# A ring of 20 weight tiles with six lent ones, and conditioning weights in loads of 1 MB

## The chip, the cores and the metric

The kernel runs on one core of a Trainium2 chip. The metric is the device time of one execution in microseconds, and the table below gives the median of three executions. One more execution was profiled; all rows shown here are from its trace.

## What is computed

One layer of a decoder trunk for 1024 tokens of width 1024, with a conditioning vector c. Token mixing is a projection into a convolution branch and a state-space (scan) branch; channel mixing is a mixture of 64 experts, of which each token uses two.

```python
mod = silu(c) @ w_ada + b_ada                       # 1024 x 6144
sh1, sc1, g1, sh2, sc2, g2 = split(mod, 6)
h = x * (1 + sc1) + sh1
conf_val, conf_gate, z, xbc, dt = split(h @ w_in)
u = silu(layer_norm(conv31(conf_val * sigmoid(conf_gate))))
y = gated_rmsnorm(ssd_scan(silu(conv4(xbc)), dt), z)
x = layer_norm(ALPHA * x + g1 * (concat(u, y) @ w_out))      # ln1
h = x * (1 + sc2) + sh2
ffn = sum over a token's two experts of gate * ((silu(h @ w1) * (h @ w3)) @ w2)
x = layer_norm(ALPHA * x + g2 * ffn)                         # ln2, the output
```

Each expert has 6 MB of weights (w1, w3, w2), 64 experts 384 MB.

## The kernel before

**Phase one** (to about 925 us). `ada_steps(r)` computes a third of `mod` each: r = 0 (sh1, sc1) at the start, since nothing goes without it, r = 1 and 2 (the other four vectors) as generators, of which `ada_more` takes a step whenever a block of projection weights is loaded. A product there has the 1024 x 2048 weights of its third as moving operand and the conditioning vector, repeated over 32 columns, as stationary one; four such products, at column offsets 0, 32, 64, 96 of the array (`tile_position`), fill the four parts of one PSUM bank. `wada` names the weight tiles, `pm` or `ada` the bank, `badd` the bias. The bank is one of a few that the projections (`mm_bank`) use too.

The tokens are worked in two halves, h = 0 and 1. `make_h(h)` transposes x and writes the modulated h as a high and a low part (hTh, hTl) in 8 tiles of 128 x 512 each. Then blocks of 128 columns of w_in are loaded (`load_block`, names wg, wv, wx, wz), split into high and low parts on ACT and POOL in the first half and kept in DRAM (`wind`) for the second, and multiplied (names pg, pv, px, pz on PE, three products for each of 8 k). Convolution taps run on DVE, the scan on PE, DVE and ACT. The out-projection passes with `wo` follow (700 to 925 us), then the routing tables (925 to 968 us), whose result for the four places that can be loaded early are the lists fix_i and fix_l.

**Expert phase** (968 to 1955 us). Expert weights come through a ring of N_RING tiles of 1 MB, loaded from SP's queue in the order of `plan`, 384 loads of 1 MB. Load n goes into tile n % N_RING and is issued when the products of load n - N_RING are done. The first N_EARLY loads need only fix_i; the next wait for fix_l. The places (experts or parts of them) are grouped into units, whose kinds stand in ORDER: F (the fixed ones), S (four places side by side, 24 loads), L (two, 12), T and H (three or one for the crowded experts). A unit gathers its tokens (`gather`, xg), transposes them (xT), multiplies with w1 (h0) and w3 (h1), joins them (s1), transposes (hT), multiplies with w2 (yp), scales by the gate (ys, yl, yh) and sends the rows to `ybuf` in DRAM. The last unit (S, number 60) does not send; its rows go through products with one-hot matrices (`hot`) straight into the last sums.

**Sums and end.** `acc` holds 8 tiles of 128 x 1024. `load_sum(i)` loads the normalized rows of phase one (`td`) from ACT's queue into tile i, multiplies by ln1's weight, adds ln1's bias (both on DVE, the vectors in l1) and scales by ALPHA on ACT. Before, one follows each of units 4 to 11. `tc.keep_in_program_order` holds its loads and its first DVE operation to the order in which the program is written; everything else is placed on its engine's queue by a scheduler. At the end `collect` gathers the rows of ybuf for each of 8 token tiles (`yb` for the first, free ring tiles for the others), and `finish` adds them to acc (DVE), sums in PSUM (z), takes statistics (BN_STATS, bs), normalizes and writes out.

The functions that the change touches, with the line numbers of the profile:

## Time and profile before

| | us |
|---|---|
| median of three executions | 2002.7 (2000.44 to 2003.66) |
| the profiled execution | 2007.87, span 2006.1 |
| phase one and routing | 0 to 968 |
| expert phase, to the last y | 968 to 1955 |
| end: last sums, normalization, output | 1955 to 2006.1 |

PE is busy 89% of the span, DVE 48%, ACT 28%, POOL 25%. A share over the whole span mixes these stages; what limits a stage is read from its own window. PE is TensorE, DVE VectorE, ACT ScalarE, POOL GpSimd, SP the engine whose queue issues most loads.

### The profile page before, as it was taken

Reading aid. Unit: us, or ns where it says so; the run is one execution under the profiler, and the core shown is the slowest. Engines: PE = TensorE matmul, PEld = TensorE weight load, DVE = VectorE, ACT = ScalarE, POOL = GpSimd, SP = SyncE. Lnnn points to the kernel's source line nnn. Section 1 sums busy time; section 2 is a strip of 40 time slices with the busy share of each in tenths; the row PEclk is TensorE's granted clock in tenths of the full one; section 3 lists DMA queues with packets and bytes.
Section 4 is the critical chain, followed back from the end, with each engine's and each line's share of the span. In section 5 each row is a group of like instructions: output and inputs, shape, how many; then the busy total and the mean of one; then the engine's idle time right before and its main releaser. Section 6 shows DMA issues by size and latency. Waiting matters only on the chain.

```text
span 2006.1 us, 23809 instructions
## 1 busy us (share of the span) xinstructions
PE 1789.1 (89%) x8136; PEld 998.1 (50%) x8136; DVE 956.2 (48%) x1928; ACT 557.4 (28%) x1054; POOL 501.6 (25%) x408
## 2 busy tenths in 40 slices
PE   6899999899999999997879799788898997999786
PEld 1566667587788777886323133232242331443233
DVE  1699999869998997867113012112011110111117
ACT  0345554643555465644100011011010010111001
POOL 0457656513443465311100001000000000000014
PEclk7899999889999999998889899999999998999998
DMA  7788888656655446674899999999989999999993
GB/s 242 234 293 265 260 254 300 223 195 212 203 190 192 160 150 221 218 289 163 316 419 419 420 415 354 419 419 420 420 300 391 419 420 419 418 412 371 419 366 161
DMA packets 202328, 620.81 MB, mean 309 GB/s; under 512 B 25886, under 2 KB 91702, under 8 KB 154332
## 3 DMA queue, kind: packets, MB, share of 16 engines
q1 hardware_dynamic: 155792, 551.74, 71.8%
q10 hardware_dynamic: 36188, 42.34, 6.6%
q0 software_dynamic: 10224, 25.18, 3.3%
q8 instruction: 65, 1.06, 0.2%
q14 instruction: 59, 0.48, 0.1%
HBM read 575.07 MB, written 79.25 MB: 326 GB/s over the span
## 4 chain that ended last, share of the span: by engine, by line
PE 45%; DMA 31%; DVE 11%; issue 5%; ACT 4%; POOL 3%; ACTq 0%; SPq 0%; DVEq 0%; POOLq 0%
DMA ring<-in_expert_w_dram 25%; PE mix L480 6%; PE px L480 5%; PE h0h L1332 3%; DVE ac L605 2%; PE pg L480 2%; PE h1h L1332 2%; PE pv L480 2%; PE pz L480 2%; PE yph L1351 2%; PE yps L1351 2%; PE ypl L1351 2%; PE h1l L1332 2%; PE h0l L1332 2%; PE ypt L1351 1%
## 5 line engine op out<-in xcount | busy, mean ns | idle before, releaser
L605 DVE SCALAR_TENSOR_TENSOR ac<-u,cw,ac 128x512 f32<-128x512 f32 x394 | 295.7, 750 | 5.5
L1294 POOL DMA_INDIRECT xg<-td,gidx x32 | 32.9, 1027 | 754.8 <-PE tph L1302 206.7
L480 PE MATMUL px<-hTh,wx_hl 128*128 128x512 f32 x512 | 169.8, 401 | 1.6 <-DVE u L619 1.2
L1332 PE MATMUL h1s<-ring,xTs 128*32 128x512 f32 x512 | 105.2, 733 | 43.2 <-DMA ring<-in_expert_w_dram 43.2
L480 PE MATMUL mix<-wo_hl,cth 128*128 128x512 f32 x416 | 129.9, 405 | 1.7 <-ACT zs L726 1.1
L1351 PE MATMUL yps<-ring,hTs 128*32 128x512 f32 x512 | 109.1, 613 | 19.3 <-DMA ring<-in_expert_w_dram 16.8
L1338 DVE TENSOR_TENSOR s1s<-s1s,h1s 128x512 f32<-128x512 f32 x8 | 5.5, 688 | 220.8 <-PE h1s L1332 220.8
L480 PEld LDWEIGHTS px<-hTh,wx_hl 128*128 128x128 f32 x512 | 95.6, 188 | 30.4 <-issue 4.6
L454 POOL TENSOR_TENSOR wo_hl<-wo,wo_hl 128x512 fp32r<-128x512 f32 x52 | 74.0, 1436 | 113.3 <-ACT wo_hl L453 106.1
L480 PE MATMUL px<-hTl,wx_hl 128*128 128x512 f32 x256 | 101.3, 396 | 0.0
L480 PE MATMUL pg<-hTh,wg_hl 128*128 128x512 f32 x256 | 89.2, 419 | 2.0 <-DVE h L520 1.8
L480 PEld LDWEIGHTS mix<-wo_hl,cth 128*128 128x128 f32 x416 | 78.2, 190 | 22.0 <-DVE wo_hl L454 1.5
L1332 PE MATMUL h0s<-ring,xTs 128*32 128x512 f32 x512 | 75.4, 639 | 14.0 <-DMA ring<-in_expert_w_dram 14.0
L311 PE MATMUL ada<-wada,cond 128*32 128x512 f32 x192 | 67.7, 706 | 19.7 <-DMA wada<-in_w_ada_dram 19.7
L480 PE MATMUL pv<-hTh,wv_hl 128*128 128x512 f32 x256 | 84.0, 396 | 0.0
L480 PE MATMUL pz<-hTh,wz_hl 128*128 128x512 f32 x256 | 83.6, 397 | 0.1
L1332 PEld LDWEIGHTS h1s<-ring,xTs 128*32 128x32 f32 x512 | 22.6, 129 | 121.0 <-DMA ring<-in_expert_w_dram 76.6
L480 PE MATMUL mix<-wo_hl,ctl 128*128 128x512 f32 x208 | 77.6, 404 | 3.1 <-DVE ctl L962 3.1
L453 ACT CAST wo_hl<-wo 128x512 fp32r<-128x512 f32 x104 | 62.9, 617 | 33.0 <-PE mix L480 18.1
L1351 PEld LDWEIGHTS yps<-ring,hTs 128*32 128x32 f32 x512 | 26.7, 111 | 87.4 <-issue 46.4
L1351 PE MATMUL ypl<-ring,hTl 128*64 128x512 f32 x256 | 66.6, 598 | 2.3 <-ACT hTl L1344 2.3
L1332 PE MATMUL h0l<-ring,xTl 128*64 128x512 f32 x256 | 63.6, 598 | 3.9 <-DMA ring<-in_expert_w_dram 3.9
(622 smaller groups left out, 3465.5 us busy)
## 6 DMA issues: line engine op xcount, KB each, us to landing
ring<-in_expert_w_dram SPq DMA_DIRECT2D x384, 1024.0 KB
wo<-in_w_out_dram SPq DMA_DIRECT2D x112, 256.0 KB
wada<-in_w_ada_dram SPq DMA_DIRECT2D x96, 256.0 KB
wind<-wx_hl SPq DMA_DIRECT2D x32, 512.0 KB
wx_hl<-wind SPq DMA_DIRECT2D x32, 512.0 KB
wind<-wg_hl SPq DMA_DIRECT2D x16, 512.0 KB
wind<-wv_hl SPq DMA_DIRECT2D x16, 512.0 KB
wx<-in_w_in_dram SPq DMA_DIRECT2D x32, 256.0 KB
```

The lines of the kernel that those rows point to most:

```text
L311: nc.tensor.matmul(pm[32 * j:32 * j + 32, :], lhs, wt, start=(k == 0), stop=(k == KT - 1), tile_position=(0, 32 * j))
L453: nc.scalar.copy(hi, wt)
L454: (eng or nc.gpsimd).tensor_tensor(lo, wt, hi, op=OP.subtract)
L480: nc.tensor.matmul(pt, lhs[a_], rhs[b_], start=(first and n == 0), stop=(last and n == 2))
L605: nc.vector.scalar_tensor_tensor(to, v_, w_, run_, op0=OP.mult, op1=OP.add)
L1294: nc.gpsimd.indirect_dma_start(out=t_, out_offset=None, in_=td, in_offset=bass.IndirectOffsetOnAxis(ap=gcol, axis=0), bounds_check=T - 1, ...
L1332: nc.tensor.matmul(hp[a:b, :], xT[:, 4 * hf + k, a:b], w_[:, k, :], start=(hf + k == 0), stop=(hf + k == 4), tile_position=(0, a))
L1338: nc.vector.tensor_tensor(s1, s1, hps[1], op=OP.mult)
L1351: nc.tensor.matmul(yps[n][a:b, :], hT[:, 2 * hf + k, a:b], w_[:, k, 512 * n:512 * n + 512], start=(hf + k == 0), stop=(hf + k == 2), tile_ ...
```

## The change

Ring: 20 tiles instead of 14, of which 14 are the ring's own and six are lent: a tile `lent`, the four halves (2 x 1024 columns x 2) of `acc`, and a tile `lend` that the last unit's one-hot matrices use. The last 44 loads (N_BACK) keep to the 14. Since acc is lent, all eight `load_sum` stand behind the unit that is third from the end. The two vectors l1 and later the first gathered rows lie in `lent` instead of `yb`. A list `slot`, `before` takes the place of n % N_RING. 16 instead of 13 loads go out on fix_i.

Conditioning: 8 loads of 1 MB for each third, with the four products of one load side by side, instead of 32 loads of 256 KB. The first third goes through the buffers of hT (four tiles of 1 MB, in which hTh and hTl now lie as slices), the second and third through one buffer `wada`, and only in the second half of the tokens. Some small loads move from ACT's queue to POOL's, the bias of the first third is loaded ahead, and the loads of mod_row wait for a store. In half 0, odd tiles of h are made with one more operation on ACT and one less on DVE.

```diff
-N_RING = 14
-N_RING_A = 8
-N_EARLY = 13
+N_RING = 20
+N_RING_A = 10
+N_EARLY = 16
+N_LEND = 6
+N_BACK = 44
...
-HA = "00000000,00000000".split(",")
+HA = "01010101,00000000".split(",")
...
         def ada_steps(r):
 
+            def load_bias():
+                t_ = wk.tile([P, 512], F32, tag="sq", bufs=SQB, name=f"badd{r}")
+                nc.scalar.dma_start(t_, bass.AP(tensor=b_ada.tensor, offset=b_ada.offset + r * 2048,
+                                                ap=[[512, 4], [0, 32], [1, 512]]))
+                return t_
+            badd = load_bias() if r == 0 else None
             pm = mm_bank(f"ada{r}")
             for k in range(KT):
+
+                if r == 0 and k != 4:
+                    wt = big.tile([P, 2048], F32, tag="hT", bufs=4, name=f"wada{r}_{k}")
+                else:
+                    wt = wk.tile([P, 2048], F32, tag="wada", bufs=1, name=f"wada{r}_{k}")
+                nc.sync.dma_start(wt, w_ada[k * P:(k + 1) * P, r * 2048:(r + 1) * 2048])
                 lhs = cond[:, k:k + 1].to_broadcast([P, 32])
-                for q in range(2):
-                    for j in (2 * q, 2 * q + 1):
-
-                        pool, tag, bufs = ([(wst, "w", WB)] * (1 if r else WB)
-                                           + [(cat, "cu", 8)] * 8 + [(cat, "cy", 8)] * 8)[0 if r else (4 * k + j) % (WB + 16)]
-                        wt = pool.tile([P, 512], F32, tag=tag, bufs=bufs, name=f"wada{r}_{k}{j}")
-                        nc.sync.dma_start(wt, w_ada[k * P:(k + 1) * P, r * 2048 + j * 512:r * 2048 + (j + 1) * 512])
-                        nc.tensor.matmul(pm[32 * j:32 * j + 32, :], lhs, wt,
-                                         start=(k == 0), stop=(k == KT - 1), tile_position=(0, 32 * j))
+                for j in range(4):
+                    nc.tensor.matmul(pm[32 * j:32 * j + 32, :], lhs, wt[:, 512 * j:512 * j + 512],
+                                     start=(k == 0), stop=(k == KT - 1), tile_position=(0, 32 * j))
```

```diff
-        def ada_more(n):
-            n = n if skip[0] % 3 else 0
-            skip[0] += 1
-            while n > 0 and late:
-                if next(late[0], 0) == 0:
-                    late.pop(0)
-                n -= 1
+        def ada_more(h):
+
+            if h == 1 and late and next(late[0], 0) == 0:
+                late.pop(0)
 
...
+    lent = rt2.tile([P, 2048], F32, name="lent")
...
+        ring += [ringb.tile([P, 2048], F32, name=f"ring{j}") for j in range(N_RING_A, N_RING - N_LEND)]
+        ring += [lent] + [acc[:, 2 * j:2 * j + 2, :].rearrange("p a d -> p (a d)") for j in range(4)] + [None]
         load_fixed(ring, N_RING_A, N_EARLY, fix_i)
...
+        ring[N_RING - 1] = wk.tile([P, 2048], F32, tag="lend", bufs=1, name="lend")
...
         def load_sum(i):
 
             if i == 0:
-                l1_ = wk.tile([P, 2, D], F32, tag="yb", bufs=1, name="l1")
-                l1[:] = [l1_[:, 0], l1_[:, 1]]
+                l1[:] = [lent[:, 0:D], lent[:, D:2 * D]]
                 for t_, v_ in zip(l1, (ln1_g, ln1_b)):
                     tc.keep_in_program_order(nc.scalar.dma_start(t_, bc(v_, 0, D)))
...
-                yy = wk.tile([P, 2, D], F32, tag="yb", bufs=1, name="yb") if i == 0 else spare[i].rearrange("p (k d) -> p k d", k=2)
+                yy = (spare[i] if i else lent).rearrange("p (k d) -> p k d", k=2)
                 nc.gpsimd.dma_start(yy, ybuf[2 * i * P:2 * (i + 1) * P, :].rearrange("(t k) d -> t k d", k=2))
```

```diff
-                hot = wk.tile([P, HW, P], F32R, tag="hot", bufs=1, name=f"hot{nm}_{j}")
+                held = wk.tile([P, 2048], F32R, tag="lend", bufs=1, name="held")
+                hot = held[:, 0:HW * P].rearrange("p (j t) -> p j t", t=P)
...
             for n in range(2):
-                yh, yl = (wk.tile([P, 512], F32R, tag=f"y{p_}", bufs=2, name=f"y{p_}{nm}_{n}") for p_ in "hl")
+                yh, yl = held[:, D + 512 * n:D + 512 * n + 512], yls[:, half[n]]
                 nc.scalar.copy(yh, y[:, half[n]])
                 nc.vector.tensor_tensor(yl, y[:, half[n]], yh, op=OP.subtract)
...
-                if n >= N_RING and uses[n - N_RING] > 0:
+                if before[n] is not None and uses[before[n]] > 0:
...
-                    load(ring[n % N_RING], *place_regs(r), which, hf)
+                    load(ring[slot[n]], *place_regs(r), which, hf)
...
+        slot, before = [], []
+        turn = [(s_, None) for s_ in range(N_RING)]
+        for n in range(len(plan)):
+            while n >= len(plan) - N_BACK and turn[0][0] >= N_RING - N_LEND:
+                turn.pop(0)
+            s_, b_ = turn.pop(0)
+            slot.append(s_)
+            before.append(b_)
+            turn.append((s_, n))
         emitted()
...
             unit(nm, [tiles(r) for r in places], cols_of(u))
-            if 4 <= n < 12:
-                load_sum(n - 4)
...
-        spare = [ring[(len(plan) + j) % N_RING] for j in range(N_RING)]
+            if n == len(units) - 3:
+                for i in range(8):
+                    load_sum(i)
...
+        spare = [ring[s_] for s_, _ in turn]
```

What the order of instructions on three engines shows. First PE in the second half of the tokens, before, where the projection px1_8 passes into px1_12 (name, then half 1 and the block; hTh and hTl the operands, whl the weights):

```order
L480 MATMUL px1_8_3967<-hTl1_6_3424,wx1_8_1_hl_3965 128x512
L480 MATMUL px1_8_3967<-hTh1_6_3420,wx1_8_1_hl_3965 128x512
L480 MATMUL px1_8_3967<-hTh1_7_3431,wx1_8_1_hl_3965 128x512
L480 MATMUL px1_8_3967<-hTl1_7_3435,wx1_8_1_hl_3965 128x512
L480 MATMUL px1_8_3967<-hTh1_7_3431,wx1_8_1_hl_3965 128x512
L480 MATMUL px1_12_4011<-hTh1_0_3348,wx1_12_0_hl_4001 128x512
L480 MATMUL px1_12_4011<-hTl1_0_3352,wx1_12_0_hl_4001 128x512
L480 MATMUL px1_12_4011<-hTh1_0_3348,wx1_12_0_hl_4001 128x512
```

The same place in the changed kernel (ada1 and ada2 are the banks of the second and third thirds, wada1_6 the load of k = 6):

```order
L485 MATMUL px1_8_3756<-hTh1_4_3162,wx1_8_1_hl_3754 128x512 x2
L321 MATMUL ada1_3379<-wada1_5_3619,cond_192 32x512 x4
L485 MATMUL px1_8_3756<-hTl1_4_3163,wx1_8_1_hl_3754 128x512
L485 MATMUL px1_8_3756<-hTh1_4_3162,wx1_8_1_hl_3754 128x512 x2
L485 MATMUL px1_8_3756<-hTl1_4_3163,wx1_8_1_hl_3754 128x512
L485 MATMUL px1_8_3756<-hTh1_4_3162,wx1_8_1_hl_3754 128x512
L321 MATMUL ada1_3379<-wada1_6_3629,cond_192 32x512 x4
L321 MATMUL ada1_3379<-wada1_7_3737,cond_192 32x512 x4
L321 MATMUL ada2_3791<-wada2_0_3792,cond_192 32x512 x4
L485 MATMUL px1_12_3801<-hTh1_0_3120,wx1_12_0_hl_3790 128x512
L485 MATMUL px1_12_3801<-hTl1_0_3121,wx1_12_0_hl_3790 128x512
```

Three groups of four conditioning products (wada1_6, wada1_7, wada2_0) now stand back to back between px1_8 and px1_12, five projection products behind wada1_5; each has a load of its own into the one buffer.

SP's queue at the start of the expert phase, before: ring8 to ring12 go out on fix_i, ring13 and what follows behind TENSOR_LOAD fix_l.

```order
L246 TENSOR_LOAD fix_i_105
L243 ISA
L243 DMA ring12_8652<-in_expert_w1_dram 128x2048
L246 TENSOR_LOAD fix_l_8638
L243 ISA
L243 DMA ring13_8653<-in_expert_w1_dram 128x2048
L246 TENSOR_LOAD fix_l_8638
L243 ISA
L243 DMA ring0_6719<-in_expert_w1_dram 128x2048
L246 TENSOR_LOAD fix_l_8638
```

In the changed kernel:

```order
L248 TENSOR_LOAD fix_i_105
L245 ISA
L245 DMA ring13_8488<-in_expert_w1_dram 128x2048
L245 ISA
L245 DMA lent_8465<-in_expert_w1_dram 128x2048
L245 ISA
L245 DMA acc_8464<-in_expert_w1_dram 128x2048
L248 TENSOR_LOAD fix_l_8475
L245 ISA
L245 DMA acc_8464<-in_expert_w3_dram 128x2048
L248 TENSOR_LOAD fix_l_8475
L245 ISA
```

ring13, lent and the first half of acc now stand ahead of the load of fix_l; three halves of acc and lend follow it.

ACT's queue over the last unit (s60), before: s1 and hT of the unit, the vectors of ln2, the copies of the last y, and the square root of the first statistics (rs0).

```order
L1309 ACTIVATE xTl30_12330<-tpl30_0_12331,modc_106 128x128 x4
L1337 ACTIVATE s1l30_12403<-h0l30_12349 128x512
L1344 COPY hTl30_12411<-thl30_12406 128x512
L1309 ACTIVATE xTs60_12444<-tps60_0_12445,modc_106 128x128 x4
L1337 ACTIVATE s1s60_12539<-h0s60_12463 128x512
L1590 DMA ring6_8112<-in_ln2_g_dram 128x1024
L1591 DMA ring6_8112<-in_ln2_b_dram 128x1024
L1344 COPY hTs60_12547<-ths60_12542 128x512
L1372 CAST yhs60_0_12590<-ys60_12583 128x512
L1372 CAST yhs60_1_12594<-ys60_12583 128x512
L1565 ACT_TABLE_LOAD
```

In the changed kernel, from behind the last unit's hT on (DMA acc<-td is a load of `load_sum`, ACTIVATE acc its scaling; three scalings and three loads stand ahead of this piece):

```order
L1282 DMA acc_8464<-td_86 128x1024
L1381 CAST held_12428<-ys60_12423 128x512 x2
L1285 ACTIVATE acc_8464<-acc_8464 128x1024
L1282 DMA acc_8464<-td_86 128x1024
L1285 ACTIVATE acc_8464<-acc_8464 128x1024
L1282 DMA acc_8464<-td_86 128x1024
L1285 ACTIVATE acc_8464<-acc_8464 128x1024
L1282 DMA acc_8464<-td_86 128x1024
L1285 ACTIVATE acc_8464<-acc_8464 128x1024
L1282 DMA acc_8464<-td_86 128x1024
L1285 ACTIVATE acc_8464<-acc_8464 128x1024
L1584 ACT_TABLE_LOAD
```

Loads and scalings of acc alternate there; five scalings and four loads stand behind the copies of the last y (held), ahead of the table load for the square root.

## Rows read from the trace of the kernel before

**Rows 1.** The page's slices of the span (40 equal ones), transfers only.

```profile
DMA  7788888656655446674899999999989999999993
GB/s 242 234 293 265 260 254 300 223 195 212 203 190 192 160 150 221 218 289 163 316 419 419 420 415 354 419 419 420 420 300 391 419 420 419 418 412 371 419 366 161
```

**Rows 2.** The page's chain that ended last, by line, share of the span.

```profile
DMA ring<-in_expert_w_dram 25%; PE mix L480 6%; PE px L480 5%; PE h0h L1332 3%; DVE ac L605 2%; PE pg L480 2%; PE h1h L1332 2%; PE pv L480 2%; PE pz L480 2%; PE yph L1351 2%; PE yps L1351 2%; PE ypl L1351 2%; PE h1l L1332 2%; PE h0l L1332 2%; PE ypt L1351 1%
```

**Rows 3.** Busy time by stage, with clock, DMA share and rate.

```profile
core 0: us, PE busy (x) PEld busy (x) DVE busy (x) ACT busy (x) POOL busy (x), PEclk, DMA share, GB/s
0.00:50.00 50.00, 31.20 (x82) 7.96 (x82) 5.94 (x57) 2.96 (x4) 0.87 (x8) 0.80 0.77 242
...
66.00:404.00 338.00, 316.90 (x1500) 224.44 (x1500) 297.39 (x490) 168.98 (x297) 194.88 (x152) 0.97 0.78 255
100.00:300.00 200.00, 187.27 (x883) 133.52 (x882) 187.19 (x307) 103.48 (x185) 120.43 (x93) 1.00 0.83 268
404.00:700.00 296.00, 290.53 (x1508) 232.25 (x1507) 257.37 (x483) 137.88 (x238) 103.39 (x85) 0.98 0.60 195
...
925.00:968.00 43.00, 26.06 (x154) 18.93 (x156) 25.07 (x103) 14.35 (x27) 3.25 (x3) 0.64 0.44 163
968.00:1955.00 987.00, 860.39 (x3662) 316.72 (x3662) 142.26 (x302) 90.03 (x196) 68.80 (x68) 0.97 0.99 402
```

**Rows 4.** The same view of stretches of the expert phase.

```profile
980.00:1000.00 20.00, 20.00 (x96) 7.55 (x92) 2.78 (x6) 0.81 (x2) 2.02 (x2) 1.00 1.02 418
1200.00:1240.00 40.00, 38.58 (x137) 16.01 (x138) 12.09 (x19) 6.45 (x13) 6.02 (x4) 1.00 0.88 338
1460.00:1520.00 60.00, 57.73 (x229) 24.25 (x230) 8.87 (x19) 5.78 (x13) 6.11 (x6) 1.00 0.82 298
1800.00:1840.00 40.00, 38.53 (x172) 15.49 (x170) 6.24 (x13) 3.19 (x7) 4.07 (x4) 1.00 0.91 352
1920.00:1940.00 20.00, 19.71 (x132) 7.03 (x134) 2.87 (x6) 2.59 (x6) 1.56 (x2) 1.00 0.78 292
```

**Rows 5.** Waits of SP's queue: us in total, times, longest us.

```profile
SPq L243 <- DMA ring<-in_expert_w_dram: 503.5, 254, 11.5
...
SPq L246 <- DVE fix_l L1320: 33.6, 1, 33.6
...
SPq L243 <- PE h0t6x L1332: 17.0, 2, 13.2
```

**Rows 6.** The chain in the first 70 us: start, us, what.

```profile
33.58 8.33 DMA mod_row<-in_ln_g_dram
...
41.99 2.79 DMA wada<-in_w_ada_dram
44.78 0.04 issue
44.82 3.93 PE ada L311 x6
```

**Rows 7.** Line L311 alone from 57 to 404 us, and PE's timeline (start, us).

```profile
57.00:404.00 347.00, 37.59 (x128) 5.12 (x128) 0.97 0.79 258
...
388.30 1.94 PE L311 MATMUL ada<-wada,cond 128*32 128x512 f32 x8
390.17 1.06 PE L499 MATMUL xT<-ident,x 128*128 128x128 f32 x4
391.16 1.04 PE L311 MATMUL ada<-wada,cond 128*32 128x512 f32 x2
```

**Rows 8.** Lines of load_sum (ns min/median/max), and a gather of 0.5 MB in the chain.

```profile
L1275 ACTq DMA_DIRECT2D acc<-td x8: 326/327/353, 1158.8 to 1351.7; - x8
...
L1276 DVE TENSOR_TENSOR acc<-acc,l x8: 1215/1216/1226, 1175.0 to 1378.1; 128x1024 f32<-128x1024 f32 x8
...
L1277 DVE TENSOR_TENSOR acc<-acc,l x8: 1215/1224/1226, 1176.3 to 1379.4; 128x1024 f32<-128x1024 f32 x8
...
L1278 ACT ACTIVATE acc<-acc x8: 1047/1056/1066, 1179.9 to 1380.7; 128x1024 f32<-128x1024 f32 x8
...
954.83 3.90 DMA xg<-td,gidx
```

**Rows 9.** The end: chain and DVE's timeline (start, us), and an issue with its landing.

```profile
1944.78 0.70 DVE s1s L1338
...
1955.00 0.75 DVE L1356 SCALAR_TENSOR_TENSOR ys<-yps,gslot,g_bc 128x512 f32<-128x512 f32 x1 [9.53 <-PE yps L1351]
1955.67 1.22 DVE L1556 TENSOR_TENSOR acc<-acc,yb 128x1024 f32<-128x1024 f32 x1
...
1959.80 0.69 DVE L1561 BATCH_NORM_STATS2 bs<-z 128x6 f32<-128x512 f32 x1
...
1993.76 1.77 DVE L1582 SCALAR_TENSOR_TENSOR ring<-ring,rs,ring 128x1024 f32<-128x1024 f32 x1
...
yb<-ybuf POOLq DMA_DIRECT2D x1, 1024.0 KB, 7.7
```

More of the change, by code (lines that the diff above doesn't have):

```diff
@@ L290, in load_xh @@
             xt = ok.tile([P, 4, 256], F32, tag="row", bufs=4, name=f"x{h}_{k}")
-            nc.scalar.dma_start(xt, x[h * HALF:(h + 1) * HALF, k * P:(k + 2) * P].rearrange("(i p) n -> p i n", p=P))
+            d_ = nc.scalar.dma_start(xt, x[h * HALF:(h + 1) * HALF, k * P:(k + 2) * P].rearrange("(i p) n -> p i n", p=P))
+            if h:
+                tc.keep_in_program_order(d_)
             return xt
@@ L345, in ada_late @@
                 for j, v_ in enumerate(second):
-                    nc.scalar.dma_start(mod_row[KT * j:KT * j + KT, :], v_.rearrange("(k p) -> k p", p=P))
-                    nc.scalar.dma_start(modc[:, j, :], v_.rearrange("(p k) -> p k", k=KT))
+                    with tc.issue_after(getattr(st, "ins", st)):
+                        nc.scalar.dma_start(mod_row[KT * j:KT * j + KT, :], v_.rearrange("(k p) -> k p", p=P))
+                        nc.scalar.dma_start(modc[:, j, :], v_.rearrange("(p k) -> p k", k=KT))
         def fold(v):
@@ L405, in vec @@
             return vcol[:, vo[nm] + t:vo[nm] + t + 1]
-        nc.scalar.dma_start(cw_row, conf_conv_w[0])
-        nc.scalar.dma_start(sw_row, ssm_conv_w[0].rearrange("k (t p) -> (k t) p", p=P))
+        nc.gpsimd.dma_start(cw_row, conf_conv_w[0])
+        nc.gpsimd.dma_start(sw_row, ssm_conv_w[0].rearrange("k (t p) -> (k t) p", p=P))
         dtb = csi.tile([P, HEADS], F32, name="dtb")
-        nc.scalar.dma_start(dtb, bc(ssm_dt_bias, 0, HEADS))
+        nc.gpsimd.dma_start(dtb, bc(ssm_dt_bias, 0, HEADS))
         a_bc = csi.tile([P, HEADS], F32, name="a_bc")
-        nc.scalar.dma_start(a_bc, bc(ssm_A_log, 0, HEADS))
+        nc.gpsimd.dma_start(a_bc, bc(ssm_A_log, 0, HEADS))
         nc.scalar.activation(a_bc, a_bc, AF.Exp)
@@ L467, in load_block @@
                 if hf == 0:
-                    ada_more(1)
+                    ada_more(h)
                 if h == 0:
@@ L492, in make_h @@
             tps = {}
+            quad = {}
             def transposes(k):
@@ L510, in make_h @@
                     transposes(k)
-                hi = big.tile([P, HALF], F32R, tag="hTh", bufs=8, name=f"hTh{h}_{k}")
+                if k % 4 == 0:
+                    quad = {p_: big.tile([P, 4, HALF], F32R, tag="hT", bufs=4, name=f"hT{p_}{h}_{k}") for p_ in "hl"}
+                hi, lo = (quad[p_][:, k % 4] for p_ in "hl")
                 nc.scalar.activation(hi, tps[k], AF.Identity, bias=sh1[:, k:k + 1], scale=sc1[:, k:k + 1])
@@ L515, in make_h @@
                     nc.scalar.activation(hs, hi, AF.Identity, bias=nsh1[:, k:k + 1])
-                    lo = big.tile([P, HALF], F32R, tag="hTl", bufs=8, name=f"hTl{h}_{k}")
                     nc.vector.scalar_tensor_tensor(lo, tps[k], sc1[:, k:k + 1], hs, op0=OP.mult, op1=OP.subtract)
@@ L520, in make_h @@
                     nc.vector.tensor_scalar(ht, tps[k], sc1[:, k:k + 1], sh1[:, k:k + 1], op0=OP.mult, op1=OP.add)
-                    lo = big.tile([P, HALF], F32R, tag="hTl", bufs=8, name=f"hTl{h}_{k}")
                     (nc.gpsimd if k % 2 < HLP[h] else nc.vector).tensor_tensor(lo, ht, hi, op=OP.subtract)
@@ L1178, in trunk @@
         V = nc.vector
-        ring += [ringb.tile([P, 2048], F32, name=f"ring{j}") for j in range(N_RING_A, N_RING)]
+        ring += [ringb.tile([P, 2048], F32, name=f"ring{j}") for j in range(N_RING_A, N_RING - N_LEND)]
+        ring += [lent] + [acc[:, 2 * j:2 * j + 2, :].rearrange("p a d -> p (a d)") for j in range(4)] + [None]
         load_fixed(ring, N_RING_A, N_EARLY, fix_i)
@@ L1213, in trunk @@
         b16 = lambda t_: t_[:, :, None].to_broadcast([P, 16, NU_STAT])
-        rows = acc[:, 0, :].bitcast(BF16).rearrange("p (j t) -> p j t", t=P)
+        rows = t2("rows", [P, 16, P], BF16)
         hot = t2("hot", [P, 16, NU_STAT], BF16)
@@ L1369, in unit @@
             ys = []
+            yls = wk.tile([P, D], F32R, tag="xT", bufs=BF[0], name=f"yl{nm}")
             for n in range(2):
-                yh, yl = (wk.tile([P, 512], F32R, tag=f"y{p_}", bufs=2, name=f"y{p_}{nm}_{n}") for p_ in "hl")
+                yh, yl = held[:, D + 512 * n:D + 512 * n + 512], yls[:, half[n]]
                 nc.scalar.copy(yh, y[:, half[n]])
@@ L1495, in of @@
                 uses[n] -= 1
-                return ring[n % N_RING]
+                return ring[slot[n]]
             return of
```

11 lines of the change are left out of this document (4 added, 7 removed).

## Prediction

> **What bounds the kernel now.** I read the slices of the span first. DMA sits near 419 GB/s from the twentieth slice on and far below before [rows 1], so there are two kernels in one: a first part in which the transfer engines have room, and an expert part in which they have none. The stage table says the same with engines: up to 925 us PE is busy 94 to 98% of each stage after the start, with DVE close behind in the first half of the tokens (297.39 of 338 us), while from 968 to 1955 us DMA is busy 0.99 of the time and PE 860.39 of 987 [rows 3]. The chain that ended last puts 25% of the span on the ring's transfers and most of its rest on PE [rows 2]. Inside the expert part I looked for stretches in which the transfers were not at their rate: an undisturbed 20 us moves 418 GB/s, and four stretches move 338, 298, 352 and 292 [rows 4]. There all 14 tiles were full and the next load waited for a product to free one; SP's waits name these products (one wait of 13.2 us), beside 503.5 us of plain queueing behind earlier transfers, and 33.6 us in which the load of the last fixed tile waited for the routing [rows 5].
>
> **The ring.** A 1 MB load takes 1048576 B at 419 GB/s = 2.5 us. Two things make the stream end earlier.
> (a) *Six more loads ahead.* 16 instead of 13 go out before the wait for the routing: three loads, 7.5 us, move into 925 to 968 us, where DMA is busy 0.44 [rows 3]. The other three follow at once behind that wait, before the first tile is free; they fill the 20 us around 970 us that I count at up to 7 us idle. Together 6 x 2.5 = 15 us at most; I take 14.
> (b) *The dips.* Time lost against 418: 40 us x (1 - 338/418) = 7.7; 60 x (1 - 298/418) = 17.2; 40 x (1 - 352/418) = 6.3; 20 x (1 - 292/418) = 6.0 [rows 4]. Six tiles more are 15 us of transfers to run on, and the longest wait for a product was 13.2 us [rows 5], so the first three should close but for 1 to 2 us. The fourth stays: the last 44 loads keep to 14 tiles. Gain 30 us. The sums of acc (5 MB: eight rows of 0.5 MB and two vectors) leave the middle of the stream and about 3 MB of them join its end; I count that as zero.
> Together -44 us. Bounds: (a) alone at half would give -30 with partly closed dips; everything, with the middle freed of 5 MB, -55.
>
> **The start.** The 32 loads of 256 KB with the other early transfers move at 242 GB/s over 50 us [rows 3], 12.1 MB; at 418 they need 29 us. The last products of the first conditioning third are at 44.82 to 48.75 us behind the last of its loads, and mod_row, two steps ahead of it in the chain, is one of a line of small ACT transfers which the change moves to POOL's queue or behind a store [rows 6]. I take -20 us; bounds 0 (other small transfers take over) and -22.
>
> **Conditioning products in the first half of the tokens.** 128 products of the second and third thirds leave this stage; they hold PE 37.59 us [rows 7]. They don't come back in full, since DVE is busy 187.19 of 200 us from 100 to 300 us, with the taps of the convolution above all [rows 3]. I take -20, between -13 (DVE sets the pace at once) and -37.
>
> **The same products in the second half.** There are 16 groups of four now. Eight products in a row took 1.94 us and two took 1.04 [rows 7], so a group of four is 1 us: +16 us on a stage in which PE is busy 290.53 of 296 us [rows 3]. Then the single buffer: a load can start only when the four products of the one before are done. The order listings of PE show three places where a group waits for a load that its predecessor lets go, with no projection or almost none between them to cover it. A round trip there costs a 1 MB load: 0.5 MB landed in 3.90 us [rows 8], and 0.5 MB more at 419 GB/s makes 5.2. Three are +15. Elsewhere 20 or more projection products of 0.4 us stand between two groups and cover it. The last chunk of the first half's scan now stands wholly ahead of the second half's projections instead of between them: I put +2 on it, an estimate from the 5.5 us that PE idles in that stage now. The bias and vector loads cost nothing on POOL's queue: POOL is busy 0.87 us of the first 50 [rows 3].
> *Phase one together:* -20 - 20 + 16 + 15 + 2 = -7 us, bounds -35 and +20.
>
> **The tail.** Here the change costs. Before, the eight sums of acc were loaded between 1158 and 1381 us under the weight stream [rows 8]. Now acc is lent to the ring, and all eight come behind the unit before the last but one. The order listings of ACT show how they lie there: load, scale, load, scale, each load queued behind the scaling of the tile before, which waits for two DVE operations, which wait for the load. Acc 0 to 2 start before the last products are over. Acc 2's load stands behind the last unit's s1, which in the trace is 10 us before the last y at 1955.00 (call that time T) [rows 9]; it lands about T - 1 between the last weights, and its scaling is done at T + 1.5. From there one tile takes 0.33 (issue) + 3.9 (landing of 0.5 MB) + 1.22 + 1.22 + 1.06 = 7.7 us [rows 8]. Acc 3 to 6 make 31 us, acc 7 needs 6.7 to the end of its DVE sum: T + 39. Only then is the lent tile free (it holds the two vectors of that sum), so the first gathered rows of y, which now land in it, start there: 7.7 us for 1 MB [rows 9], a sum of 1.2, and the first statistics come at T + 48 instead of T + 4.8. From the first statistics to DVE's last end took 35.7 us, with six sums of 1.21 in it that are now over before; that leaves 28 to 29, and then 10.6 us to the end of the span as before [rows 9]. End at T + 87.5 instead of T + 51.1: +36 us. Bounds: with landings of 2.5 us instead of 3.9 and a gather of 5, +26; if acc 2 lands late behind the weights, +42.
> The Trainium skill (DMA: Bandwidth & Descriptors, "Anatomy of one DMA") gives a transfer 2.0 us and its bytes at 436 GB/s: by it 0.5 MB lands in 3.2 us and 1 MB in 4.4 when alone, an estimate by which the tail would be about 7 us shorter and the three round trips 2. Rows 8 have 3.90 for a gather, so I keep the rows.
>
> **Sum.** -44 - 7 + 36 = -15. The profiled execution took 2007.9 us (span 2006.1), 5.2 over the median of 2002.7; I take the difference, so 2007.9 - 15 = 1993 for such an execution and 1987.5 on the scale of the median. A difference under 0.2% (4 us) can't be told from no change.
>
> **Rivals.**
> 1. *The chain of sums is mostly hidden* (17%): some last load holds T back while acc goes on, or ACT runs its loads earlier than I place them. Then the tail costs some 10 us: -44 - 7 + 10 = -41, 1962. For it: nothing else uses the transfers by then. Against: the order on ACT is fixed, and five scalings stand behind the copies of the last y.
> 2. *Every conditioning load shows* (13%): SP takes its queue in order, and a conditioning load that waits for PE holds the projection weights behind it. 15 loads at 5.2 instead of three are +62 more: 2050; at half of that, 2018. It decides from 15 us more, 1.25 us for each of the other twelve loads. For it: SP already waits for tiles at every step. Against: 8 us or more of products between most groups.
> The Trainium skill (Trainium Kernel Development and Optimization, "Best Practices") asks for two buffers so that transfer and work overlap, which speaks for this rival; no run here shows it yet for this buffer.
> 3. *The ring does less than it says* (8%): the dips are set by PE (busy 38.58 of 40 and 57.73 of 60 us in them [rows 4]) and not by tiles. Then only the 14 us of (a) come in: -14 - 7 + 36 = +15, 2018.
> 4. *My forecast*, 1972 to 2000 (62%); 10 of these 62 lie within 4 us of no change.
>
> **How the numbers follow.** The likeliest is 1987. The range reaches down into rival 1 and up to the near cases of 2 and 3: 1958 to 2011. Faster by over 0.2%: 17 + 52 = 0.69; within: 10 and 1 of the mild cases of 2 and 3, 0.11; slower: the rest of these two, 0.20.
>
> **What would show it.** Right: ring transfers near 419 GB/s at the places of the three dips; the last y about 50 us earlier than 1955; first statistics 40 us or more after it, with ACT's waits on acc's DVE sums between them; PE waiting for the conditioning loads three times some 5 us between 400 and 500 us; the first projection before 50 us. Wrong: dips that stay with PE full (rival 3), waits for a conditioning load at most groups (2), statistics at T + 15 (1), or a start that does not move, since it needs all the loads to be limited by their size.

## The result and the profile after

The changed kernel takes 2054.6 us (median of four, 2053.07 to 2055.54) against 2003.2 for the kernel before (median of four): ratio 1.026, interval 1.0244 to 1.0276. The forecast was 1987, range 1958 to 2011. The profiled execution has a span of 2053.8 us. Its slices, transfers only, which answer to [rows 1]:

```profile
span 2053.8 us, 23602 instructions
...
DMA  9777774487765536675899999999979999989862
GB/s 321 220 223 228 237 257 146 137 297 236 249 207 188 187 131 213 203 284 218 323 419 420 420 420 400 422 419 420 408 294 419 420 420 419 416 356 418 347 241 85
```

Two holes are new: 146 and 137 GB/s around 310 to 410 us, and the end. The start is better (321 instead of 242). Busy time by stage of the changed kernel, cut at its own milestones:

```profile
core 0: us, PE busy (x) PEld busy (x) DVE busy (x) ACT busy (x) POOL busy (x), PEclk, DMA share, GB/s
0.00:50.00 50.00, 22.00 (x112) 9.30 (x113) 11.28 (x67) 10.37 (x16) 13.83 (x25) 0.86 0.98 324
50.00:335.00 285.00, 269.65 (x1286) 212.93 (x1287) 268.18 (x440) 158.14 (x275) 180.44 (x139) 0.96 0.72 231
335.00:408.00 73.00, 42.41 (x219) 31.22 (x217) 48.41 (x109) 31.99 (x59) 28.06 (x24) 0.65 0.33 112
408.00:718.00 310.00, 288.09 (x1485) 215.30 (x1486) 238.55 (x419) 121.06 (x206) 90.71 (x73) 0.96 0.68 227
...
994.00:1962.00 968.00, 847.91 (x3690) 312.19 (x3686) 131.37 (x297) 86.79 (x194) 66.73 (x68) 0.96 0.98 403
1962.00:2010.00 48.00, 24.23 (x54) 11.23 (x48) 24.04 (x23) 7.80 (x8) 0.53 (x1) 0.72 0.44 172
```

The same stretches of the kernel before, from its first projection to the end of the second half's projections:

```profile
66.00:373.00 307.00, 293.38 (x1393) 210.31 (x1394) 276.19 (x452) 152.60 (x268) 175.80 (x136) 0.99 0.81 264
373.00:404.00 31.00, 23.52 (x112) 14.12 (x107) 21.20 (x39) 16.38 (x29) 19.08 (x16) 0.79 0.53 174
404.00:691.00 287.00, 282.11 (x1468) 227.31 (x1468) 248.48 (x469) 132.24 (x229) 99.74 (x82) 0.98 0.61 198
```

The third line of the changed kernel and the second of this fence are the same passage, from the last gate product (pz) of the first half to the first projection (pg) of the second. It took 31 us and takes 73, with PE busy 42 of them at a granted clock of 0.65.

All profiled executions, cut at the same milestones on PE (first pg; last pz of half 0; first pg and last pz of half 1; last mix; first product of the expert phase; last yps; first statistics; end). Columns are durations in us, from one execution each; stages that an experiment leaves alone differ by up to 4 us between them (the second half of the changed kernel and of experiments 2 to 5: 309.8 to 313.6):

| kernel | start | half 0 | passage | half 1 | out-proj. | routing | expert | to statistics | finish |
|---|---|---|---|---|---|---|---|---|---|
| before | 65.9 | 306.7 | 31.7 | 286.5 | 232.9 | 36.9 | 995.1 | 4.0 | 46.3 |
| changed | 49.8 | 285.7 | 72.5 | 309.8 | 237.4 | 38.5 | 968.8 | 47.4 | 43.8 |
| 1 x free | 53.7 | 286.7 | 30.7 | 317.0 | 241.2 | 37.9 | 969.5 | 45.2 | 44.5 |
| 2 sums together (ACT) | 50.8 | 288.2 | 71.3 | 312.9 | 240.1 | 36.4 | 988.9 | 6.7 | 45.7 |
| 3 units in order | 50.2 | 288.6 | 71.5 | 311.1 | 236.5 | 36.4 | 960.2 | 46.3 | 44.3 |
| 4 conditioning alone | 51.3 | 287.7 | 74.0 | 310.3 | 237.8 | 37.8 | 993.9 | 4.0 | 46.8 |
| 5 sums from SP | 49.9 | 286.7 | 73.4 | 313.6 | 239.0 | 35.3 | 971.6 | 7.3 | 46.1 |
| 6 without the reloads | 51.0 | 289.7 | 75.8 | 280.0 | 233.1 | 36.3 | | | |
| 7 ring mended | 65.9 | 305.7 | 30.3 | 284.4 | 236.0 | 36.6 | 966.6 | 5.7 | 45.7 |
| 8 all mended | 54.3 | 287.8 | 31.1 | 318.2 | 241.1 | 38.1 | 962.7 | 5.7 | 46.4 |
| 9 ring and start | 57.3 | 304.5 | 25.8 | 285.4 | 236.1 | 35.3 | 962.8 | 5.7 | 47.0 |

From the first two lines: start -16.1, first half -21.0, passage +40.8, second half +23.3, out-projection +4.5, routing +1.6, expert stage -26.3, wait for the first statistics +43.4, finish -2.5; together +47.7, the difference of the spans.

**The passage.** The change has a line that the prediction did not cost: the loads of x for the second half are held behind all ACT work that is written ahead of them.

```diff
         def load_xh(h, k):
             xt = ok.tile([P, 4, 256], F32, tag="row", bufs=4, name=f"x{h}_{k}")
-            nc.scalar.dma_start(xt, ...)
+            d_ = nc.scalar.dma_start(xt, ...)
+            if h:
+                tc.keep_in_program_order(d_)
```

The issues of these eight loads (four for each half) in the changed kernel, from the view of one source line (ns min/median/max, first and last start in us):

```profile
L293 ACTq DMA_DIRECT2D x<-in_x_dram x8: 374/460/720, 0.7 to 399.4; - x8
```

and in the kernel before:

```profile
L291 ACTq DMA_DIRECT2D x<-in_x_dram x8: 385/491/1252, 0.7 to 58.4; - x8
```

The first of the four held loads and the first transposes that use it, in the changed kernel (start, us):

```profile
383.93 0.47 ACTq L293 DMA_DIRECT2D x<-in_x_dram  x1
388.73 1.04 PE L505 MATMUL xT<-ident,x 128*128 128x128 f32 x8
```

Before, x was there 320 us ahead; its transposes and h filled the gaps of the first half's last normalization. Now they start at 388.7, when this is over, and the second half's first projections have nothing to work on until 407.9. In the meantime PE does the rest of the first half's scan: it is busy 42 us in the passage where it was busy 24. Before, some of that work stood between the second half's projections.

**The second half.** PE's timeline at the three groups that stand back to back (start, us, ..., idle time before):

```profile
456.81 1.07 PE L321 MATMUL ada<-wada,cond 128*32 128x512 f32 x8
465.94 1.94 PE L321 MATMUL ada<-wada,cond 128*32 128x512 f32 x8 [6.71 <-DMA wada<-in_w_ada_dram]
472.87 1.93 PE L321 MATMUL ada<-wada,cond 128*32 128x512 f32 x8 [4.99 <-DMA wada<-in_w_ada_dram]
480.14 1.94 PE L321 MATMUL ada<-wada,cond 128*32 128x512 f32 x8 [5.34 <-DMA wada<-in_w_ada_dram]
```

Three round trips of 5.0 to 6.7 us, 17.0 together. A group of four is 8 instructions in the trace, two for each product, and takes 1.07 us, or 1.94 behind a wait. All groups of this stage, 15 of the 16 (the first one runs just before it):

```profile
408.00:718.00 310.00, 19.04 (x120) 2.55 (x120) 0.96 0.68 227
```

The prediction read "x8" in [rows 7] as eight products and "x128" as 128; they are four and 64. Its price of 1 us for a group was half of what that row shows, 1.94 us, and came out near the 1.07 us of most groups by luck.

**The dips.** The stretches that answer to the second to fourth of [rows 4], in the changed kernel:

```profile
1200.00:1240.00 40.00, 38.82 (x150) 15.61 (x149) 6.14 (x13) 3.19 (x7) 3.02 (x3) 1.00 1.01 415
1460.00:1520.00 60.00, 57.41 (x204) 23.03 (x203) 8.34 (x16) 5.27 (x12) 5.05 (x5) 1.00 0.76 304
...
1800.00:1860.00 60.00, 50.77 (x241) 18.83 (x240) 8.15 (x16) 5.27 (x12) 5.04 (x5) 0.94 0.91 364
```

and one of SP's waits there (us in total, times, longest us):

```profile
SPq L245 <- PE ypt6x L1358: 28.3, 2, 26.1
```

The first dip nearly closed: 7.7 us were lost before, now 0.3 in the same window and 1.4 behind it (the expert phase starts 33 us later, and 1240 to 1260 us moved 388 GB/s). The second, 60 x (1 - 304/418) = 16.4, and the third, 7.8, did not. SP waits 26.1 us for the last products of a crowded expert's third part (t6x). Their transposes (tht6x) and the products on PE, in the kernel before:

```profile
1475.09 0.75 PE L1342 MATMUL tht6x<-ident,s1t6x 128*128 128x128 f32 x4 [0.85 <-DVE s1t6x L1338]
...
1476.57 7.09 PE L1351 MATMUL ypt6x<-ring,hTt6x 128*64 128x512 f32 x32 [0.29 <-ACT hTt6x L1344]
```

in the changed kernel, and SP's queue behind them:

```profile
1476.93 0.75 PE L1349 MATMUL tht6x<-ident,s1t6x 128*128 128x128 f32 x4 [0.85 <-DVE s1t6x L1345]
...
1500.70 7.04 PE L1358 MATMUL ypt6x<-ring,hTt6x 128*64 128x512 f32 x32
...
1504.33 14.99 SPq L245 DMA_DIRECT2D ring<-in_expert_w_dram  x10
```

Before, the products ran 1.5 us behind their transposes, ahead of the next unit. In the changed kernel the scheduler put the next two units' first products ahead of them, and they ran 24 us behind, with the tiles they read held and the ring's queue blocked behind the first of them.

**The start of the expert phase.** The first 40 us behind its first product, before and in the changed kernel:

```profile
960.70:1000.70 40.00, 38.69 (x173) 13.93 (x172) 4.91 (x12) 5.28 (x11) 3.01 (x3) 0.95 0.87 349
...
993.70:1033.70 40.00, 38.03 (x177) 14.09 (x177) 5.52 (x12) 5.22 (x11) 3.00 (x3) 0.98 1.01 412
```

Against 418 GB/s that is 6.6 us lost before and 0.6 now. From the first product to the last yps 367 expert loads were issued instead of 370, and four loads of acc instead of eight.

**The tail.** ACT's timeline behind the last unit's transposes (start, us):

```profile
1956.25 1.06 ACT L1285 ACTIVATE acc<-acc 128x1024 f32<-128x1024 f32 x1 [0.94 <-DVE acc L1284]
1956.26 0.33 ACTq L1282 DMA_DIRECT2D acc<-td  x1
1962.44 0.62 ACT L1381 CAST held<-ys 128x512 fp32r<-128x512 f32 x1 [5.13 <-DVE ys L1363]
...
1968.31 1.06 ACT L1285 ACTIVATE acc<-acc 128x1024 f32<-128x1024 f32 x1 [0.51 <-DVE acc L1284]
1968.38 0.33 ACTq L1282 DMA_DIRECT2D acc<-td  x1
1979.99 1.06 ACT L1285 ACTIVATE acc<-acc 128x1024 f32<-128x1024 f32 x1 [10.62 <-DVE acc L1284]
1979.99 0.33 ACTq L1282 DMA_DIRECT2D acc<-td  x1
1986.03 1.06 ACT L1285 ACTIVATE acc<-acc 128x1024 f32<-128x1024 f32 x1 [4.98 <-DVE acc L1284]
...
1998.07 1.06 ACT L1285 ACTIVATE acc<-acc 128x1024 f32<-128x1024 f32 x1 [5.07 <-DVE acc L1284]
```

The chain is there, link by link. T, the time of the last y, is now 1961.66. At its end the chain that ended last goes through the gather into the lent tile and PE's sums:

```profile
1998.33 5.05 DMA lent<-ybuf
2003.38 0.04 issue
2003.42 3.78 PE z L1568 x4
```

The first statistics, from DVE's timeline, answer to the line at 1959.80 in [rows 9]:

```profile
2003.40 1.23 DVE L1575 TENSOR_TENSOR acc<-acc,lent 128x1024 f32<-128x1024 f32 x1 [3.02 <-DMA lent<-ybuf]
2009.92 2.49 DVE L1580 BATCH_NORM_STATS2 bs<-z 128x6 f32<-128x512 f32 x4 [5.30 <-PE z L1579]
```

### The profile page after: what moved, and what is told of

Same layout as the page of the kernel before. It is cut to its first block, busy times and chain, and to the rows that moved or that the text cites. A ratio compares the mean times of both kernels' runs of the same rounds, so it can differ in the third digit from the quotient of the medians.

```text
span 2053.8 us, 23602 instructions
## 1 busy us (share of the span) xinstructions
PE 1762.4 (86%) x8136; PEld 1004.3 (49%) x8136; DVE 953.1 (46%) x1924; ACT 563.6 (27%) x1060; POOL 503.5 (25%) x418
## 4 chain that ended last, share of the span: by engine, by line
PE 39%; DMA 30%; DVE 5%; issue 4%; POOL 2%; ACT 1%; SPq 0%; ACTq 0%; POOLq 0%; DVEq 0%
DMA ring<-in_expert_w_dram 16%; PE mix L485 7%; DMA lend<-in_expert_w_dram 5%; DMA acc<-in_expert_w_dram 5%; PE px L485 3%; PE yph L1358 2%; PE pg L485 2%; PE h0l L1339 2%; PE pv L485 2%; PE h1l L1339 2%; PE ypt L1358 1%; PE pz L485 1%; PE h0h L1339 1%; PE h0t L1339 1%; PE h1h L1339 1%
## 5 line engine op out<-in xcount | busy, mean ns | idle before, releaser
L1358 PE MATMUL yps<-ring,hTs 128*32 128x512 f32 x400 | 81.0, 611 | 14.3 <-DMA ring<-in_expert_w_dram 10.3
L1339 PE MATMUL h1s<-ring,xTs 128*32 128x512 f32 x368 | 71.0, 703 | 19.4 <-DMA ring<-in_expert_w_dram 19.3
L635 POOL TENSOR_TENSOR tap<-tap,tap 128x512 f32<-128x512 f32 x38 | 52.0, 1369 | 69.6 <-ACT tap L633 68.4
L1339 PE MATMUL h0s<-ring,xTs 128*32 128x512 f32 x368 | 56.3, 621 | 9.5 <-DMA ring<-in_expert_w_dram 8.8
L750 POOL TENSOR_TENSOR dec<-ab,future 128x512 f32<-128x512 f32 x32 | 43.1, 1346 | 83.0 <-DMA ab<-acsd 62.6
L1345 DVE TENSOR_TENSOR s1h<-s1h,h1h 128x512 f32<-128x512 f32 x8 | 5.5, 688 | 121.9 <-PE h1h L1339 121.9
L485 PEld LDWEIGHTS pg<-hTh,wg_hl 128*128 128x128 f32 x256 | 50.6, 199 | 18.2 <-issue 2.0
L1345 DVE TENSOR_TENSOR s1l<-s1l,h1l 128x512 f32<-128x512 f32 x8 | 5.5, 688 | 109.6 <-PE h1l L1339 109.6
```

The lines of the kernel that those rows point to most:

```text
L485: nc.tensor.matmul(pt, lhs[a_], rhs[b_], start=(first and n == 0), stop=(last and n == 2))
L635: nc.gpsimd.tensor_tensor(side, side, tmp, op=OP.add)
L750: nc.gpsimd.tensor_tensor(dec, ab, future[:, None, :].to_broadcast([P, 4, P]), op=OP.add)
L1339: nc.tensor.matmul(hp[a:b, :], xT[:, 4 * hf + k, a:b], w_[:, k, :], start=(hf + k == 0), stop=(hf + k == 4), tile_position=(0, a))
L1345: nc.vector.tensor_tensor(s1, s1, hps[1], op=OP.mult)
L1358: nc.tensor.matmul(yps[n][a:b, :], hT[:, 2 * hf + k, a:b], w_[:, k, 512 * n:512 * n + 512], start=(hf + k == 0), stop=(hf + k == 2), tile_ ...
```

## The experiments

Times are medians on the chip of the run, ratios to the kernel before on the same chip.

**1. The loads of x free.** The two lines `if h: tc.keep_in_program_order(d_)` are taken out.

> The changed kernel, but the four loads of x for the second half of the tokens are no longer held behind the ACT work that is written ahead of them. Theory 1 (the pinned loads make the passage between the halves long: x arrives at 384 us and later, so the transposes start at 389 instead of beside the end of the first half): the passage from the last gate projection of the first half to the first projection of the second falls from 72 us to 30 to 40, and the time from 2054.6 to 2015 to 2025. Rival 1 (the passage is long because the conditioning products that filled it are gone, and the end of the scan and the normalization has to be waited for anyway): passage over 60 us, time 2045 to 2055.

Measured 2029.9 us, ratio 1.0125 (1.0089 to 1.0161). The passage is 30.7 us, as theory 1 says; the time missed 2015 to 2025. The gain of 42 us is given back in part: the last chunk of the first half's scan now lies in the second half again (317.0 instead of 309.8), the four loads of x go out between 19 and 52 us beside the conditioning loads (start 53.7 instead of 49.8), and the out-projection is 3.8 longer. The span falls by 27.3 us. The stretch of the passage:

```profile
340.00:371.00 31.00, 19.38 (x86) 12.78 (x84) 26.61 (x47) 18.00 (x32) 16.74 (x15) 0.69 0.25 86
```

Rival 1 falls: with one group of conditioning products in it instead of the three before, the passage is as short as before.

**2. The sums' loads together.**

```diff
-            tc.keep_in_program_order(nc.scalar.dma_start(acc[:, i, :], td[i * P:(i + 1) * P, :]))
+            if i == 0 or over:
+                for j in ([i] if over else range(8)):
+                    tc.keep_in_program_order(nc.scalar.dma_start(acc[:, j, :], td[j * P:(j + 1) * P, :]))
```

(`over` is set only where the sums are made again behind experts that overflow.)

> The changed kernel, but the eight loads of acc are issued one behind the other ahead of the first scaling, instead of each behind the scaling of the tile before. Theory 2 (a chain of load, two DVE sums and scaling makes the tail): from the last product of the last unit to the end 50 to 58 us instead of 91, the time 2014 to 2023. Rival 2 (the tail is long because the rows of y that are gathered into the lent tile come late, or because all eight sums need DVE and ACT there): a tail of 75 us or more, the time 2038 to 2055.

Measured 2037.6 us, ratio 1.0151 (1.0117 to 1.0186). From the last product to the end it is 52.4 us instead of 91.2, as theory 2 says, but the expert stage is 20 us longer and the time was missed. The new wait, from the view of waits of 1900 to 1960 us:

```profile
ACT xTl L1318 <- DMA ring<-in_expert_w_dram: 38.0, 1, 38.0
...
PE h0l L1341 <- ACT xTl L1318: 26.8, 1, 26.8
```

and the issue on ACT's queue:

```profile
1913.63 20.11 ACTq L1284 DMA_DIRECT2D acc<-td  x8
```

Eight loads needed 20.1 us to be issued amid the ring's loads, with ACT's copy of the next unit's tokens queued behind them, and PE waited 26.8 us for that copy. That the queue is the cause, and not the 5 MB, is shown only by experiment 5.

**3. Units in order.**

```diff
+                            with tc.issue_after(yp_last[0].ins) if yp_last and nm != "ov" else nullcontext():
+                                nc.tensor.matmul(hp[a:b, :], xT[:, 4 * hf + k, a:b], w_[:, k, :], start=(hf + k == 0),
...
-                            nc.tensor.matmul(yps[n][a:b, :], hT[:, 2 * hf + k, a:b], w_[:, k, 512 * n:512 * n + 512],
...
+                            yp_last[:] = [nc.tensor.matmul(
...
```

> The changed kernel, but the first products of each unit stand behind the last products of the unit before on PE's queue. Theory 3 (the second dip of the transfers stays because the last products of a crowded expert stand 24 us later on PE than before and hold their tiles, behind which the whole ring waits): the rate between 1480 and 1520 us rises from 228 and 261 to over 350 GB/s, SP's longest wait for these products falls from 26 us to under 12, and the time to 2040 to 2047. Rival 3 (PE sets the pace there whatever the order is): the dip moves by under 3 us, time within 4 us of 2054.6. Loss that both allow: a few us of gaps on PE between units where it has nothing else.

Measured 2045.2 us, ratio 1.0193 (1.0154 to 1.0231); the expert stage is 960.2 instead of 968.8. SP's longest wait for these products fell to 10.6 us, and 1480 to 1520 us moved 321 GB/s where the changed kernel moved 228 and 261 in its halves:

```profile
1480.00:1520.00 40.00, 36.14 (x120) 15.77 (x122) 7.82 (x16) 4.58 (x11) 6.03 (x6) 0.96 0.86 321
```

Theory 3 holds for the place, the wait and the time, but the rate stayed under the 350 that it named: of 16.6 us lost in this window 7.3 came back. The third dip shrank too, from 7.8 us to 3.0:

```profile
1800.00:1860.00 60.00, 54.60 (x274) 20.78 (x273) 7.66 (x16) 5.18 (x12) 5.04 (x5) 0.97 0.98 397
```

So the order is somewhat under half of the second dip. For the rest the prediction's rival 3, PE's pace, is not excluded: in the changed kernel PE was busy 57.41 of the 60 us there.

**4. Conditioning alone**, on the kernel before.

> The kernel before with the conditioning part of the change alone (the loads of 1 MB, groups of four, the loads that move between queues, the slices of hT), the ring left at 14 tiles and the sums where they were. If the parts add up: phase one longer by 33 us as in the changed kernel, time 2030 to 2040. Rival (the ring's early loads are what lengthens phase one): within 8 us of 2003.

Measured 2041.9 us, ratio 1.0172 (1.0136 to 1.0207). Its stages up to the expert phase are those of the changed kernel within 2 us each; the time is 2 us over the range, since phase one grew by 38 us and not by 33. The parts add up, and the ring has no share in the passage.

**5. The sums from SP's queue.** As in experiment 2, with `nc.sync.dma_start` for the vectors and the eight loads.

> The changed kernel, but the two vectors and the eight loads of acc are issued together from SP's queue, at the place between the ring's loads where the program reaches them, ahead of the first DVE sum. In the run with the loads together on ACT's queue the tail fell by 41 us, but PE stood still for 27 us, since ACT's copy of the next unit's tokens was queued behind eight loads that each waited for an earlier transfer. Theory 4 (only the queue was wrong): the expert stage stays within 8 us of the changed kernel's 968.8, the first statistics come under 8 us after the last product, time 2015 to 2026. Rival 4 (5 MB at this place cost the weight stream 20 us from whatever queue): expert stage 980 or more, time 2033 or more.

Measured 2024.5 us, ratio 1.0098 (1.0073 to 1.0123). Expert stage 971.6, statistics 7.3 us behind the last product: theory 4. The loads were issued over 13 us among the ring's, and only loads stood behind them on this queue:

```profile
L1284 SPq DMA_DIRECT2D acc<-td x8: 319/320/431, 1922.1 to 1935.3; - x8
```

**6. Without the reloads.** `wada1_0` is loaded once, and all groups of the second and third thirds read it. This leaves out 15 loads, so four conditioning vectors hold other values, other tokens go to other experts, and what follows the routing is not compared.

> The changed kernel with 15 of the 16 loads of the second and third conditioning thirds left out (all their products take the first of these loads). Theory 5 (three back-to-back groups wait a round trip each, 17 us in the trace, and the rest is hidden): the second half of the tokens, 309.8 us from its first to its last projection, falls to 288 to 296, time 2034 to 2042. Rival 5a (the loads hold SP's queue and with it the projection weights, so they cost much more): a fall of over 28 us. Rival 5b (DVE sets the pace there): under 6 us.

Measured 2289.2 us; that is no answer to the forecast of 2034 to 2042, since with other tokens at the experts the time behind the first statistics is 311.5 us instead of 43.8. The second half of the tokens took 280.0 us instead of 309.8:

```profile
416.00:696.00 280.00, 279.14 (x1468) 214.40 (x1461) 234.27 (x412) 125.53 (x210) 89.60 (x72) 1.00 0.62 195
```

That is 30 us, but three of the groups, which no load holds any more, moved ahead into the passage, which took 75.8 us instead of 72.5. Over both stages the fall is 26.5 us: more than the 17.0 of the three waits and the 14 to 22 of theory 5, and under the 28 of rival 5a. Neither holds as it was set. PE is busy 279.14 of 280 us at a clock of 1.00, against 288.09 of 310 at 0.96. So 21 of the 30 us are idle time of PE, and 9 busy time: the three groups at 1.94 instead of 1.07 us are 2.6 of it, the three that moved about 3, and the cause of the rest is not shown. Whether some of the idle time beside the three waits came from SP's queue, which stood 39.8 us waiting for these products between 404 and 500 us, the runs don't separate.

**7. The ring mended**: the ring part alone on the kernel before, with 3 and 5.

> The kernel before with the ring part of the change alone, the sums of acc loaded from SP's queue, and the first products of a unit behind the last ones of the unit before. If the ring is worth what its parts showed: phase one as before (968 us), expert stage 995 - 26 (six tiles) - 9 (order of units) + 4 = 964, tail as before within 4 us, time 1968 to 1982. Rival (the ring gained because phase one handed over later): expert stage 985 or more, time 1992 or more.

Measured 1976.9 us, ratio 0.9858 (0.9833 to 0.9883), at the number: phase one as before, expert stage 966.6, tail 51.4.

**8. All mended**: the changed kernel with 1, 3 and 5.

> The changed kernel with the loads of x free, the sums from SP's queue and the units in order. If the stages add up: start -13, first half -19, passage -1, second half +29, out-projection +5, so phase one within 8 us of before; expert stage and tail as in the ring alone mended; time 1970 to 1988, within 8 us of that run. Rival (conditioning costs more than it gives when the passage overlaps, as 317 us for the second half and 53.7 for the start hint): 10 us or more above the ring alone.

Measured 1988.3 us, ratio 0.9918 (0.9888 to 0.9947), 11 us above the ring alone, where the forecast had at most 8. The rival holds: against experiment 7, start and first half give 29.5 us, the second half takes 33.8, and out-projection and routing 6.6.

**9. Ring and start.** Experiment 7 with the first conditioning third as in the change; the other two stay in loads of 256 KB among the first half's products. With it come the small loads on POOL's queue (but for the five of vrow, which stay on ACT's), the wait of mod_row's loads and the extra ACT operation for odd tiles of h.

```diff
+                if r == 0:
+                    if k != 4:
+                        wt = big.tile([P, 2048], F32, tag="hT", bufs=4, name=f"wada{r}_{k}")
+                    else:
+                        wt = wk.tile([P, 2048], F32, tag="wada", bufs=1, name=f"wada{r}_{k}")
+                    nc.sync.dma_start(wt, w_ada[k * P:(k + 1) * P, r * 2048:(r + 1) * 2048])
...
+                        if r:
+                            wt = wst.tile([P, 512], F32, tag="w", bufs=WB, name=f"wada{r}_{k}{j}")
+                            nc.sync.dma_start(wt, w_ada[k * P:(k + 1) * P, r * 2048 + j * 512:r * 2048 + (j + 1) * 512])
```

> The mended ring (six lent tiles, sums from SP's queue, units in order) with only the first third of the conditioning as in the change: its eight loads of 1 MB, the small loads on POOL's queue, the slices of hT. The second and third thirds stay in loads of 256 KB among the products of the first half, and the loads of x stay free. If the start's gain is apart from the rest: first projection at 50 to 54 us instead of 65.9, first half 303 to 309 us, passage and second half as before, time 11 to 15 us under the mended ring's 1977, 1960 to 1968. Rival (the start's gain is taken back in the first half, where DVE and PE are both nearly full): within 4 us of 1977.

Measured 1960.7 us (1958.74 to 1961.96), ratio 0.9779 (0.9754 to 0.9804), the best of all. The first projection came at 57.3, 8.6 us earlier than without it and later than expected, and the passage was 4.5 us shorter besides. The rival falls. Which of the edits that came along has which share is not shown. The slices of this kernel, transfers only:

```profile
GB/s 320 234 278 278 285 246 283 206 209 228 194 199 190 147 159 214 213 326 182 351 419 420 420 419 400 420 419 421 419 356 417 420 420 420 419 416 399 411 290 203
```

## Why the prediction was wrong

**The start and the first half were right**: -16 and -21 where the sum had -20 and -20. About 4 us of the start are no gain of the larger loads: they come from the loads of x that left it, and with these back (experiment 1) the start takes 53.7 us.

**The passage is the step that failed.** The prediction put "+2" on "the last chunk of the first half's scan", with 5.5 us of PE's idle time as its measure. The passage grew by 41 us. The cause is not the scan but the loads of x, which were not in the sum; experiment 1 frees them and the passage is back at 30.7. Over the whole kernel that is worth 27 us, since part of the scan then goes back into the second half. The order of x's transposes on PE, behind the whole normalization and most of the scan, stood in the program's order before the run; the prediction read that order for the scan and did not ask what the transposes waited for.

**The dips were over-sized.** "Should close but for 1 to 2 us" gave 30 us; the three dips lost 31.2 before and about 26 now. The step counted tiles (15 us of cover against a wait of 13.2) and took the order of the products that free them as given. It was not: ypt6x now stood 24 us behind its transposes, and one blocked load stopped SP's queue; when it went, ten loads followed within 15 us. Experiment 3 shortens the stage by 9 us. Rival 3 had this place with PE's pace as the cause, and for what experiment 3 leaves it stands open. The rest of the -26.3: (a), put at 14, shows as three loads fewer in the stage (7.5 us) and 6.0 us less lost in its first 40 us, and the four loads of acc that left the stage (2.1 MB) are 5 us of transfer, which the sum had at zero. About 3 us are left without a cause.

**The tail was right in cause, and in size partly by luck**: first statistics at T + 48 as forecast, end at T + 92 (T + 87.5). Its links were off both ways, and the errors cancel to the first statistics: acc 3 was loaded 7 us earlier than the sum had it; its cycle and the next took 12.1 and 11.6 us, with loads that DVE could use only 8.4 and 9.1 us after their issue while the seven gathers of y were under way; the others took 6.0 instead of 7.7; the gather 5.05 instead of 7.7; and between it and the first statistics stand 6.5 us of PE's products, where the sum had 1.2 of DVE, in a stretch with the clock at 0.72. From the first statistics to the end it took 43.8 us instead of 39. The gather's 5.05 us lie nearer to the rule of the Trainium skill (DMA: Bandwidth & Descriptors, "Anatomy of one DMA"), 4.4 us for 1 MB, than to the row that the sum took. The page gives this rule for transfers issued by GpSimd, as the gather is; the loads of acc from ACT's queue are not, though the prediction put both under it.

**The second half**: +16 and +15 were forecast; the trace has 19.0 of groups and 17.0 of three waits, so both terms were near, and PE waited at three groups and not at most of them, as rival 2 had it. That the stage grew by 23 and not by 36 is the other side of the passage: about 13 us of the first half's scan and normalization, which PE did here before, it now does there. Experiment 6 puts the loads at 26.5 us over both stages, so they cost up to 9 us beyond the three waits, which the prediction put at nothing. What the Trainium skill's wish for two buffers (Trainium Kernel Development and Optimization, "Best Practices") could bring in these two stages is bounded by these 26.5 us; two buffers were not tried.

The sum, with what was measured: -16 - 21 + 41 + 23 + 6 - 26 + 41 = +48 instead of -15. Of the 63 us between them, passage and second half are 31 (64 instead of 33), the expert stage 18, out-projection and routing, which the sum left out, 6, the tail 5 and start and first half 3.

## What to carry to other kernels

Read the order of a changed kernel for the loads too: an instruction pinned behind its engine's earlier work takes all its users along, and what it costs stands where they start. A deeper ring that is served in order is worth only what the order of its readers leaves; when the tiles grow, check that no reader moved back. And put a batch of loads on a queue behind which no work of an engine waits: the same eight loads cost 20 us from ACT's queue and 3 from SP's.

## What was not expected of the hardware

Eight loads on ACT's queue took 20.1 us to be issued while the weight stream ran at 420 GB/s; the issue of one took 0.33 us elsewhere. The trace names the landing of a ring load as what released ACT; the runs don't show why an issue on ACT's queue had to wait for it. Four products that took 1.07 us took 1.94 behind idle times of 6.71, 4.99 and 5.34 us, three times in a row, in stretches with a mean granted clock of 0.91 and 0.75; the ratio is near that of TensorE's two levels, 2.4 and 1.2 GHz, but no row gives the clock of such a group alone.
